# A 32-slot expert, a new order of expert blocks and units, combines in other PSUM banks, and cross attention by all heads at once

## The chip, the cores and the metric

The kernel runs on one core of a Trainium2 chip. The metric is the device time of one execution in microseconds, from the start of the program to its end; lower is better. One execution computes the whole model for one sequence of 256 tokens. Every weight is float32 and is read from HBM once for each use.

## The reference, cut to what matters

Two blocks of two layers each run one after the other, on a sequence of 256 tokens with 1024 features. Layer 0 of the first block isn't touched. Its layer 1 ends in a mixture of 8 experts, each token going to 2 of them:

```
def moe_swiglu(u, router_w, w1, w3, w2):
    top_vals, top_idx = lax.top_k(u @ router_w, 2)
    gates = softmax(top_vals)
    ...  # sorted by expert
    y[e] = (silu(x[e] @ w1[e]) * (x[e] @ w3[e])) @ w2[e]    # w1, w3: 1024 x 2816, w2: 2816 x 1024
    return sum of gates * y over the token's experts
```

Each layer of the second block mixes tokens, adds cross attention to a memory of 256 rows, and ends in 16 experts in groups, of which a token takes two:

```
q = z[..., last 512 columns]                   # z = x @ w_in
s = einsum('bshd,bmhd->bhsm', q, k) * 128 ** -0.5     # 4 heads of 128
o = einsum('bhsm,bmhd->bshd', softmax(s), v)
x = layer_norm(ALPHA * x + concat([tok, o]) @ w_out)
h = silu(xt @ w_gate[e]) * (xt @ w_up[e])      # 1024 x 512 each, 16 experts
out = out + combine[:, e:e + 1] * (h @ w_down[e])
```

`tok` is a spatial gating unit in the first of these layers and a short convolution in the second.

## The kernel before

**The stream of weights.** All large weights come through `raw` (L195 to L203): it takes the next slot of a ring of SBUF slots, and SyncE (SP) issues one DMA into it, of 1024 KB or 768 KB. A slot can be loaded again once TensorE (PE) has done the last matmul that reads it, so an SP that runs ahead waits at the next `dma_start` for PE, and everything behind it on SP waits too.

**Layer 1's experts** (`moe_layer1`). The tokens of an expert are gathered into a fixed number of slots. The first expert is expert 0; the others follow by the number of their tokens. The first five have 96 slots, the last three 64 (`NL = 5`). The columns of one expert's hidden width are cut into three blocks of 1024, 1024 and 768, and a unit (q, i) is block i of the q-th expert. `up` (matmuls at L1234) multiplies the gathered tokens by w1 and w3: with 64 slots, the output of 64 rows uses half of PE's columns, so two matmuls into different halves of the array run side by side; with 96 slots the work is cut into groups of 32 columns, four side by side. `turn` (L1259) transposes the hidden values through PE, and `down` (L1280) multiplies by w2 into `y`, whose banks stay reserved for the expert. PSUM has three banks "g" for `up`, three "y" for `y`, and two "b" for everything small. `combine` (L1285 to L1309) takes a finished expert's `y`, splits it in two terms by ScalarE (`yh`) and VectorE (`yl`), multiplies by the transposed selection on PE and adds the gated result to `macc` on VectorE. Each of its two halves has four matmuls.

The order on PE is written by hand: a unit's `up`, then the `down` of the unit before, then its own `turn`. Two streams of experts, the 96-slot ones and the 64-slot ones, are merged by what remains of each. Where an expert has just finished, half 0 of its combine stands before the `down` of that place and half 1 behind it, in "b" banks.

**Block 2** (`block2`). The layer's input is transposed; `gemm_T` and `gemm_N` multiply by w_in, each weight split in two terms by ScalarE and VectorE (L255, L256) ahead of its matmuls. The generator `cross` (L1504 to L1532) does a head at a time: scores (`xs`), softmax on ScalarE and VectorE (`xp`), transposes (`xpT`), the product with v (`xo`). Two heads are asked for ahead of the last gemm and two behind it; a scheduler places their instructions between those of the gemm. Then w_out, a layer norm, and the router.

**Block 2's experts**. 16 experts are put into seven units of 128 slots. Units 0, 1, 3 and 4 are two experts with 64 slots (12 pieces of weights each), unit 2 is one expert with 128 slots (6 pieces), unit 5 one with 64 and two with 32 (18 pieces), unit 6 four with 32 (24 pieces). They run in this order: the `up` of a unit (L1748), the `down` of the one before (L1774), the combine of the one before that (L1787). The first 16 pieces of the stage are loaded during the mixing ahead of it.

Of the kernel before, what the change touches and what calls it, by code (L numbers as in the profile page):

```python
# [37 lines left out]
KEX = 4  # L38
CAPS = (64,) * KEX + (128,) + (64,) * 5 + (32,) * 6
NL = 5  # L40
# [115 lines left out]
class Net:  # L156
# [1014 lines left out]
    def moe(self, E, F, uh, oh0, rank, slot, gates, w1, w3, w2, acc, mp):  # L1171
# [15 lines left out]
        class Job:  # L1187
# [29 lines left out]
            def up(j, i):  # L1217
# [3 lines left out]
                nb = 3 if m == 96 else 2  # L1221
                ps = [self.bank("up", "g") for _ in range(nb)]

                if m == 96:
                    t, plan = 32, [(0, 0, 0, 0, 0), (0, 1, 0, 0, 32), (0, 2, 0, 0, 64), (0, 3, 0, 1, 64),
                                   (1, 0, 0, 1, 0), (1, 1, 0, 1, 32), (1, 2, 1, 1, 0), (1, 3, 1, 1, 32),
                                   (2, 0, 1, 0, 0), (2, 1, 1, 0, 32), (2, 2, 1, 0, 64), (2, 3, 1, 1, 64)]
                else:
                    t, plan = 64, [(0, 0, 0, 0, 0), (0, 1, 1, 0, 0), (1, 0, 0, 1, 0), (1, 1, 1, 1, 0)]
# [9 lines left out]
                if m == 96:  # L1239
                    parts = [((0, 96), A, (0, 0), (2, 0)), ((0, 64), B, (1, 0), (1, 64)), ((64, 96), B, (0, 96), (2, 96))]  # L1240
                else:
                    parts = [((0, 64), A, (0, 0), (0, 64)), ((0, 64), B, (1, 0), (1, 64))]
# [20 lines left out]
            def down(j, i):  # L1263
# [6 lines left out]
                if m == 96:  # L1270
                    t, one = 32, [(0, 0, 0, 0), (0, 1, 0, 32), (0, 2, 0, 64), (0, 3, 1, 64)]
                    plans = one + [(1, 0, 1, 0), (1, 1, 1, 32)], [(1, 2, 1, 0), (1, 3, 1, 32)] + one
                else:
                    t, plans = 64, ([(0, 0, 0, 0), (0, 1, 1, 0)],) * 2
                v = j.w2[f0:f0 + n, :].rearrange("(p k) d -> p k d", k=nk)
                for k2 in range(0, nk, 2):
                    x = self.raw(v[:, k2:k2 + 2, :], 2, D)
                    for k in range(k2, k2 + 2):
                        for b, c, o, s in plans[k % 2]:
                            nc.tensor.matmul(j.y[b][c * t:(c + 1) * t, :], hT[:, k, s:s + t],  # L1280
                                             x[:, k - k2, o * 512:(o + 1) * 512],
                                             start=(i == 0 and k == (k % 2 if b else 0)), stop=(i == len(blocks) - 1 and k >= nk - 2),
                                             tile_position=(0, c * t), skip_group_check=True)

            def combine(j, halves=(0, 1)):  # L1285
                m, y = j.m, j.y
                for o in halves:
                    js = slice(o * 512, (o + 1) * 512)
                    src = y[0][:m]
                    if o:  # L1290
# [10 lines left out]
                    for tt in range(2):  # L1301
                        p = self.bank("comb")
# [30 lines left out]
        def job(q):  # L1333
# [3 lines left out]
            m = 96 if q < NL else 64  # L1337
# [8 lines left out]
        with tc.manual_schedule(engines={mybir.EngineType.PE}):  # L1346
# [3 lines left out]
            for u, (q, i) in enumerate(units):  # L1350
# [5 lines left out]
                if out is not None:  # L1356
                    jobs[out].combine((0,))
# [18 lines left out]
        nc.vector.tensor_scalar(capv, rank, float(NL), 32.0, op0=OP.is_lt, op1=OP.mult)  # L1376
        nc.vector.tensor_scalar(capv, capv, 64.0, None, op0=OP.add)
        over = mp.tile([128, E], F32, name="over")
# [636 lines left out]
```

## Time and profile before

| | us |
|---|---|
| median of 3 runs (2153.97 to 2158.74) | 2156.89 |
| the profiled execution, its own time | 2155.77 |
| its span in the trace | 2153.9 |
| layer 1's experts, first `up` to last `macc` | 761.9 to 1456 |
| block 2, first layer: mixing and routing | 1456 to 1568 |
| block 2, first layer: experts | 1568 to 1796 |
| block 2, second layer: mixing and routing | 1796 to 1913 |
| block 2, second layer: experts, then the end | 1913 to 2153.9 |

The span is what the trace shows between its first and its last instruction; the execution's own time is 1.9 us longer. The mean granted clock of TensorE was 0.965 of full speed. TensorE is busy for 92% of the span, VectorE for 39%, ScalarE for 27%. The transfers moved 634.57 MB, 294 GB/s over the span, but this mean hides stages with 187 GB/s (the first 762 us) and with over 400.

### The profile page before, as it was taken

How to read it: one execution, taken by the hardware profiler on the slowest of the kernel's cores; microseconds unless marked ns; L12 is line 12 of the kernel's file. 1: busy time of each engine (PE TensorE's matmuls, PEld its weight loads, DVE VectorE, ACT ScalarE, POOL GpSimd, SP SyncE). 2: the span in 40 equal slices, each digit the busy share in tenths (PEclk: the TensorE clock that was granted, in tenths of full speed). 3: DMA queues.
4: the chain of work that ended last, by engine and by line, in shares of the span. 5: the costliest groups of instructions: out<-in, count | busy, mean ns of one | idle time of the engine just before them, and what ended most of it. 6: DMA issues, size and time to landing. Idle time of an engine off the chain costs nothing. (4 is left out here: it accounts for less than half of the span.)

```text
span 2153.9 us, 32324 instructions
## 1 busy us (share of the span) xinstructions
PE 1982.9 (92%) x13265; PEld 1102.5 (51%) x13265; DVE 831.4 (39%) x1703; ACT 577.9 (27%) x973; POOL 82.9 (4%) x121
## 2 busy tenths in 40 slices
PE   6999897999889899999999999998799997989996
PEld 2777665889867533333333333337643425843431
DVE  4464476445778601101211111017632315652223
ACT  3353254334533411101101011015321212522210
POOL 1010100000130000000000000001000001000000
PEclk9999998999999999999999999998899998989998
DMA  7532557784532679999999999976589898479996
GB/s 293 182 119 111 196 176 262 262 274 145 182 100 84 232 290 368 395 410 411 411 390 411 411 408 414 411 308 222 191 340 384 362 421 333 154 304 401 377 391 249
DMA packets 166339, 634.57 MB, mean 295 GB/s; under 512 B 11952, under 2 KB 53040, under 8 KB 124192
## 3 DMA queue, kind: packets, MB, share of 16 engines
q1 hardware_dynamic: 163808, 630.76, 76.2%
q8 instruction: 111, 1.82, 0.3%
q0 software_dynamic: 2080, 1.04, 0.2%
q10 hardware_dynamic: 288, 0.52, 0.1%
q14 instruction: 52, 0.43, 0.1%
HBM read 631.20 MB, written 1.05 MB: 294 GB/s over the span
## 5 line engine op out<-in xcount | busy, mean ns | idle before, releaser
L1234 PE MATMUL up<-raw,xg 128*32 128x512 f32 (+3 forms) x3456 | 403.6, 560 | 0.0
L256 DVE TENSOR_TENSOR wh<-raw,wh 128x1024 fp32r<-128x1024 f32 x182 | 221.3, 1222 | 180.2 <-ACT wh L255 179.0
L1234 PEld LDWEIGHTS up<-raw,xg 128*32 128x32 f32 (+1 forms) x3456 | 133.0, 115 | 255.0 <-issue 248.5
L255 ACT ACTIVATE wh<-raw 128x1024 fp32r<-128x1024 f32 x182 | 190.8, 1058 | 231.6 <-PE gT L192 88.3
L1748 PE MATMUL up<-raw,xg 128*64 128x512 f32 (+1 forms) x1088 | 207.8, 601 | 4.5 <-DMA raw<-in_w_up 2.9
L1280 PE MATMUL y<-raw,hT 128*32 128x512 f32 (+1 forms) x1584 | 208.6, 608 | 0.0
L1246 DVE TENSOR_TENSOR h<-up,h 64x512 f32<-64x512 f32 (+5 forms) x63 | 40.8, 647 | 390.3 <-ACT h L1244 389.5
L1774 PE MATMUL y<-raw,hT 128*64 128x512 f32 (+1 forms) x576 | 133.4, 597 | 8.9 <-DMA raw<-in_w_down 4.1
L1244 ACT ACTIVATE h<-up 64x512 f32<-64x512 f32 (+5 forms) x63 | 35.0, 555 | 371.5 <-PE up L1234 371.0
L1280 PEld LDWEIGHTS y<-raw,hT 128*32 128x32 f32 (+1 forms) x1584 | 60.2, 116 | 139.2 <-issue 126.8
L1748 PEld LDWEIGHTS up<-raw,xg 128*64 128x64 f32 (+1 forms) x1088 | 63.5, 129 | 132.8 <-issue 124.6
L1754 DVE TENSOR_TENSOR h<-up,h 64x512 f32<-64x512 f32 x28 | 29.6, 1056 | 192.2 <-ACT h L1753 192.1
L190 PE MATMUL gT<-fuTh,wh 128*128 128x256 f32 x352 | 101.0, 287 | 0.0
L191 PE MATMUL gT<-fuTl,wh 128*128 128x256 f32 x352 | 99.6, 283 | 0.0
L192 PE MATMUL gT<-fuTh,wh 128*128 128x256 f32 x352 | 99.5, 283 | 0.0
L445 PE MATMUL mod<-raw,cs 128*32 128x512 f32 x384 | 63.0, 693 | 26.0 <-DMA raw<-in_l_mod_w 26.0
L1774 PEld LDWEIGHTS y<-raw,hT 128*64 128x64 f32 (+1 forms) x576 | 38.4, 124 | 94.1 <-issue 65.1
L1753 ACT ACTIVATE h<-up 64x512 f32<-64x512 f32 x28 | 30.0, 1071 | 193.1 <-PE up L1748 193.1
L190 PEld LDWEIGHTS gT<-fuTh,wh 128*128 128x128 f32 x352 | 67.4, 191 | 12.1 <-issue 10.9
L192 PEld LDWEIGHTS gT<-fuTh,wh 128*128 128x128 f32 x352 | 67.5, 192 | 0.4
L191 PEld LDWEIGHTS gT<-fuTl,wh 128*128 128x128 f32 x352 | 67.4, 192 | 0.2
L1260 ACT COPY hT<-hT 128x384 f32<-128x384 f32 (+1 forms) x24 | 10.5, 438 | 165.2 <-PE hT L1259 142.5
(577 smaller groups left out, 3173.4 us busy)
## 6 DMA issues: line engine op xcount, KB each, us to landing
raw<-in_l_moe_w SPq DMA_DIRECT2D x216, 1024.0 KB, 12.8
raw<-in_w_gate SPq DMA_DIRECT2D x64, 1024.0 KB, 8.8
raw<-in_w_up SPq DMA_DIRECT2D x64, 1024.0 KB, 9.3
raw<-in_w_down SPq DMA_DIRECT2D x64, 1024.0 KB, 12.0
raw<-in_l_mod_w SPq DMA_DIRECT2D x48, 1024.0 KB, 6.4
raw<-in_l_moe_w SPq DMA_DIRECT2D x64, 768.0 KB, 12.9
raw<-in_l_ffn_w SPq DMA_DIRECT2D x33, 1024.0 KB, 5.4
raw<-in_l_w_in SPq DMA_DIRECT2D x14, 1024.0 KB, 5.4
```

The lines of the kernel that those rows point to most:

```text
L190: mm(out, l[0], r[0], start=start, stop=False, skip_group_check=True)
L191: mm(out, l[0], r[1], start=False, stop=False, skip_group_check=True)
L192: mm(out, l[1], r[0], start=False, stop=stop, skip_group_check=True)
L255: nc.scalar.activation(hi, x[:, k:k + s, :], AF.Copy)
L256: nc.vector.tensor_tensor(lo, x[:, k:k + s, :], hi.bitcast(F32), OP.subtract)
L445: nc.tensor.matmul(p[32 * j:32 * j + 32, :], self.cs[:, k, :], x[:, 0, j * 512:(j + 1) * 512], start=(k == 0), stop=(k == KC - 1), tile_po ...
L1234: nc.tensor.matmul(ps[b][c * t:(c + 1) * t, :hn], j.xg[:, k, s:s + t], x[w][:, k - k2, half * hn:(half + 1) * hn], start=(k == 0), stop=(k ...
L1244: nc.scalar.activation(h[a:z, js], ps[b1][o1:o1 + z - a, :hn], AF.Silu)
L1246: nc.vector.tensor_tensor(h[a:z, js], ps[b3][o3:o3 + z - a, :hn], h[a:z, js], OP.mult)
L1280: nc.tensor.matmul(j.y[b][c * t:(c + 1) * t, :], hT[:, k, s:s + t], x[:, k - k2, o * 512:(o + 1) * 512], start=(i == 0 and k == (k % 2 if ...
L1748: nc.tensor.matmul(p[o:o + t, :], xg[:, k, c:c + t], pair[w][:, k - k4, :], start=(k == 0), stop=(k == KC - 1), tile_position=(0, o))
L1774: nc.tensor.matmul(y[o][a:a + n, :], hT[:, q * m + a:q * m + a + n], x[e][:, k, o * 512:(o + 1) * 512], start=(q == 0), stop=(q == 3), til ...
```

## The change

- The smallest expert of layer 1 has 32 slots instead of 64 (`SLOTS1`). Its `up` puts w1 and w3 by two halves into one bank, in four groups of 32 columns; its `down` adds even contraction steps into two groups and odd ones into the other two; its combine first adds these two quarters (one ScalarE copy, one VectorE add for each half).
- Layer 1's units begin with two units of the first expert instead of three before the merge, and the second stream is experts 5, 7, 6, with the 32-slot one in the middle instead of 64-slot experts 5, 6, 7.
- The combine of a finished expert moves behind `down`: half 0, then `turn`, then half 1, in the "g" banks of `up`. The last two combines stay as they are.
- Block 2's units run in the order 0, 1, 5, 3, 2, 4, 6.
- Cross attention computes the scores of all four heads into four banks and all softmaxes at the start; the probabilities lie in a slot of the ring (`room`), which goes back behind the fourth head. The heads' transposes and products with v are placed at every second step of the next gemm. In the first layer the scores move ahead of the gemm for v; the transposes `swT` and the row of logits move into the last gemm.

The core of the diff:

```diff
+UNITS = (0, 1, 5, 3, 2, 4, 6)
-NL = 5
+SLOTS1 = (96,) * 5 + (64,) * 2 + (32,)
+SECOND = (5, 7, 6)
...
-                nb = 3 if m == 96 else 2
+                nb = {96: 3, 64: 2, 32: 1}[m]
...
+                    t, plan = 32, [(0, 0, 0, 0, 0), (0, 1, 0, 1, 0), (0, 2, 1, 0, 0), (0, 3, 1, 1, 0)]
...
+                    t, plans = 32, ([(0, 0, 0, 0), (0, 1, 1, 0)], [(0, 2, 0, 0), (0, 3, 1, 0)])
...
-            def combine(j, halves=(0, 1)):
+            def combine(j, halves=(0, 1), tag="b"):
...
+                    if m == 32:
+                        src = mp.tile([128, 512], F32, tag="half", name="ysum", bufs=2)[:m]
+                        nc.scalar.copy(src, y[0][o * 32:o * 32 + 32])
+                        nc.vector.tensor_tensor(src, y[0][64 + o * 32:96 + o * 32], src, OP.add)
...
-        streams = [[(q, i) for q in qs for i in range(nb)] for qs in (range(NL), range(NL, E))]
-        units, streams[0] = streams[0][:nb], streams[0][nb:]
+        streams = [[(q, i) for q in qs for i in range(nb)] for qs in (range(SECOND[0]), SECOND)]
+        units, streams[0] = streams[0][:2], streams[0][2:]
...
                 out, done = done, None
-                if out is not None:
-                    jobs[out].combine((0,))
...
                 if out is not None:
-                    jobs.pop(out).combine((1,))
+                    jobs[out].combine((0,), "g")
                 jobs[q].turn(i)
+                if out is not None:
+                    jobs.pop(out).combine((1,), "g")
...
+        P = []
+        room, slot = self.take([128, 4, 2, 256], F32, "xp")
         for h in range(4):
             ps = self.bank("xs")
...
+            P.append(ps)
+        for h in range(4):
+            ps = P[h]
...
-            p = lp.tile([128, 2, 256], F32, tag="xp", name="xp", bufs=2)
+            p = P[h] = room[:, h]
...
+        yield
+        for h in range(4):
+            p = P[h]
             pt = self.transpose4([p[:, tt, m * 128:(m + 1) * 128] for m in range(2) for tt in range(2)], "xpT")
...
+            if h == 3:
+                self.ring.append(slot)
             yield
...
+                xs = self.cross(qT, kv, mixT, lp)
+                next(xs)
...
-                xs = self.cross(qT, kv, mixT, lp)
-                next(xs)
-                next(xs)
-                self.gemm_N(w, 0, xT, range(2), lambda i, p: nc.scalar.activation(u[:, i, :], p, AF.Gelu))
-                for _ in xs:
-                    pass
...
+                for q, _ in enumerate(self.steps_N(w, 0, xT, range(2), lambda i, p: nc.scalar.activation(u[:, i, :], p, AF.Gelu))):
+                    if q % 2:
+                        next(xs)
...
+        units = [units[i] for i in UNITS]
```

Three places show how instructions move. The first is TensorE in layer 1's experts where the first expert has just finished; `up` and `y` are the matmuls of `up` and `down`, `hT` the transposes of `turn`, `comb` those of a combine. Before:

```order
L1234 MATMUL up<-raw,xg 64x512 x32
L1304 MATMUL comb<-yh,oht 128x512
L1304 MATMUL comb<-yl,oht 128x512
L1304 MATMUL comb<-yh,oht 128x512
L1304 MATMUL comb<-yl,oht 128x512
L1280 MATMUL y<-raw,hT 32x512 x48
L1304 MATMUL comb<-yh,oht 128x512
L1304 MATMUL comb<-yl,oht 128x512
L1304 MATMUL comb<-yh,oht 128x512
L1304 MATMUL comb<-yl,oht 128x512
L1259 MATMUL hT<-cst,h 128x64 x8
L1234 MATMUL up<-raw,xg 32x512 x96
```

And after, at the same place:

```order
L1238 MATMUL up<-raw,xg 32x512 x96
L1288 MATMUL y<-raw,hT 64x512 x16
L1316 MATMUL comb<-yh,oht 128x512
L1316 MATMUL comb<-yl,oht 128x512
L1316 MATMUL comb<-yh,oht 128x512
L1316 MATMUL comb<-yl,oht 128x512
L1265 MATMUL hT<-cst,h 128x96 x8
L1316 MATMUL comb<-yh,oht 128x512
L1316 MATMUL comb<-yl,oht 128x512
L1316 MATMUL comb<-yh,oht 128x512
L1316 MATMUL comb<-yl,oht 128x512
L1238 MATMUL up<-raw,xg 64x512 x32
```

The two halves of the combine stood on either side of the long run of `y`; now only the eight transposes of `hT` lie between them, and the next `up` follows at once. A 64-slot unit also stands a unit earlier.

The second place is TensorE in the first mixing of block 2, in the gemm ahead of w_out; `gN` are the gemm's matmuls, `xs`, `xpT` and `xo` those of one head of the cross attention. Before:

```order
L334 MATMUL xpT<-cst,xp 128x128 x4
L190 MATMUL gN<-wh,xTh 128x512
L191 MATMUL gN<-wh,xTh 128x512
L192 MATMUL gN<-wh,xTl 128x512
L190 MATMUL gN<-wh,xTh 128x512
L191 MATMUL gN<-wh,xTh 128x512
L192 MATMUL gN<-wh,xTl 128x512
L1530 MATMUL xo<-xpTs,mem_4833 128x256 x2
L1512 MATMUL xs<-mem_4833,bq 128x256 x2
```

After, for the second head; the scores of all heads (`xs`, eight matmuls in a row) now stand before the gemm for v, straight behind that for q:

```order
L336 MATMUL xpT<-cst,xp 128x128 x4
L192 MATMUL gN<-wh,xTh 128x512
L193 MATMUL gN<-wh,xTh 128x512
L194 MATMUL gN<-wh,xTl 128x512
L192 MATMUL gN<-wh,xTh 128x512
L193 MATMUL gN<-wh,xTh 128x512
L194 MATMUL gN<-wh,xTl 128x512
L1552 MATMUL xo<-xpTs,mem_4833 128x256 x2
L192 MATMUL gN<-wh,xTh 128x512
```

A head's product with v is no longer followed by the next head's scores, and all four heads lie within the gemm; before, the last two lay within the matmuls of w_out.

The third place is SyncE in block 2's first expert stage, behind the 16 pieces loaded ahead: four `w_down` pieces of unit 0, and what follows. `TENSOR_LOAD` reads the number of an expert whose weights are picked by count, and an `ISA` row belongs to the DMA behind it. Before:

```order
L200 DMA raw<-in_w_down 128x2048 x4
L1799 TENSOR_LOAD idx
L1799 ISA x2
L200 ISA
L200 DMA raw<-in_w_gate 128x2048
L200 ISA
L200 DMA raw<-in_w_up 128x2048
L200 ISA
L200 DMA raw<-in_w_gate 128x2048
L200 ISA
L200 DMA raw<-in_w_up 128x2048
L200 DMA raw<-in_w_down 128x2048 x4
```

After:

```order
L202 DMA raw<-in_w_down 128x2048 x4
L1824 TENSOR_LOAD idx
L1824 ISA x2
L1824 TENSOR_LOAD idx
L1824 ISA x2
L1824 TENSOR_LOAD idx
L1824 ISA x2
L202 ISA
L202 DMA raw<-in_w_gate 128x2048
L202 ISA
L202 DMA raw<-in_w_up 128x2048
```

Before, one expert's four pieces for `up` follow, then the `w_down` of unit 1; now the numbers of three experts are read, and twelve pieces for their `up` come before the `w_down` of unit 1.

## Rows read from the trace of the kernel before

**Rows 1.** The page, busy time and share of TensorE over the span.

```profile
PE 1982.9 (92%) x13265; PEld 1102.5 (51%) x13265; DVE 831.4 (39%) x1703; ACT 577.9 (27%) x973; POOL 82.9 (4%) x121
```

**Rows 2.** By stage: start:end, length, busy PE, PEld, DVE, ACT, POOL; clock, DMA share, GB/s.

```profile
761.90:836.00 74.10, 71.51 (x677) 24.49 (x680) 6.58 (x11) 5.46 (x10) 0.00 (x0) 0.98 0.85 323
836.00:1433.00 597.00, 588.00 (x4636) 209.88 (x4630) 82.07 (x136) 61.23 (x118) 0.00 (x0) 0.99 1.01 406
...
1585.00:1735.00 150.00, 140.61 (x698) 59.29 (x696) 41.39 (x67) 32.06 (x43) 0.00 (x0) 1.00 0.95 387
1735.00:1789.00 54.00, 47.37 (x259) 13.62 (x262) 9.46 (x14) 4.79 (x6) 5.14 (x8) 1.00 1.01 419
...
1930.00:2079.00 149.00, 140.59 (x695) 58.99 (x694) 40.62 (x66) 32.03 (x43) 0.00 (x0) 1.00 0.95 387
```

**Rows 3.** The same view, windows of 100 us within layer 1's experts.

```profile
900.00:1000.00 100.00, 99.27 (x790) 35.98 (x784) 10.51 (x18) 6.68 (x13) 0.00 (x0) 1.00 1.02 411
1000.00:1100.00 100.00, 96.80 (x734) 33.54 (x734) 18.37 (x30) 12.70 (x24) 0.00 (x0) 0.98 1.00 400
...
1300.00:1400.00 100.00, 99.62 (x748) 34.51 (x738) 12.19 (x19) 8.77 (x16) 0.00 (x0) 1.00 1.02 412
```

**Rows 4.** Waits of SP's DMA queue, 761.9 to 1456: us, times, longest.

```profile
SPq L200 <- PE up L1234: 315.5, 126, 9.2
...
SPq L200 <- DMA raw<-in_l_moe_w: 20.6, 19, 2.0
```

**Rows 5.** Groups of PE by shape, 761.9 to 1456: busy us, mean ns, idle before.

```profile
L1234 PE MATMUL up<-raw,xg 128*64 128x512 f32 x384 | 83.7, 594 | 0.0
...
L1280 PE MATMUL y<-raw,hT 128*64 128x512 f32 x264 | 58.6, 596 | 0.0
...
L1234 PE MATMUL up<-raw,xg 128*64 128x384 f32 x192 | 31.6, 488 | 0.0
```

**Rows 6.** Timeline of PE, `up` of a 96-slot and a 64-slot unit: start, us.

```profile
1161.09 20.81 PE L1234 MATMUL up<-raw,xg 128*32 128x512 f32 x192
...
1281.01 13.95 PE L1234 MATMUL up<-raw,xg 128*64 128x512 f32 x64
```

**Rows 7.** Timeline, sum of two parts of `y` in layer 1's last combine.

```profile
1450.05 0.58 ACT L1293 COPY ysum<-y 64x512 f32<-64x512 f32 x1 [12.52 <-PE y L1280]
1450.67 0.68 DVE L1295 TENSOR_TENSOR ysum<-y,ysum 64x512 f32<-64x512 f32 x1 [9.33 <-ACT ysum L1293]
```

**Rows 8.** Waits of PE, 761.9 to 1456: us, times, longest.

```profile
PE xg L1208 <- DVE macc L1308: 4.1, 4, 2.0
...
PE hT L1259 <- DVE macc L1308: 1.9, 5, 0.4
```

**Rows 9.** Timeline of PE, end of block 2's first experts; in brackets the wait before.

```profile
1783.76 1.90 PE L1774 MATMUL y<-raw,hT 128*32 128x512 f32 x4 [0.44 <-DMA raw<-in_w_down]
1786.25 1.90 PE L1774 MATMUL y<-raw,hT 128*32 128x512 f32 x4 [0.59 <-DMA raw<-in_w_down]
1788.73 3.62 PE L1774 MATMUL y<-raw,hT 128*32 128x512 f32 x20 [0.58 <-DMA raw<-in_w_down]
```

**Rows 10.** The page, DMA issues: count, KB each, median us to landing.

```profile
raw<-in_w_gate SPq DMA_DIRECT2D x64, 1024.0 KB, 8.8
```

**Rows 11.** Loads by SP, 1425 to 1573: ns min/median/max, first and last start.

```profile
L200 SPq DMA_DIRECT2D raw<-in_w_up x8: 327/328/340, 1483.1 to 1556.3; - x8
```

**Rows 12.** Waits of PE in block 2's first mixing, 1456 to 1568.

```profile
PE xo L1530 <- ACT xpTs L1527: 1.9, 2, 1.2
PE xpT L334 <- DVE xp L1524: 1.4, 1, 1.4
```

**Rows 13.** Timeline of ACT behind the gemm for q in that mixing.

```profile
1479.51 1.38 ACT L1548 ACTIVATE bq<-gT 128x256 f32<-128x256 f32 x4 [1.05 <-PE gT L192]
```

**Rows 14.** Waits of PE in block 2's second mixing, 1796.3 to 1913.

```profile
PE xpT L334 <- DVE xp L1524: 0.4, 2, 0.2
```

**Rows 15.** Timeline of PE, `up` of four 32-slot experts in block 2.

```profile
1738.39 11.35 PE L1748 MATMUL up<-raw,xg 128*32 128x512 f32 x96
```

More of the change, by code (lines that the diff above doesn't have):

```diff
@@ L1281, in down @@
                                              x[:, k - k2, o * 512:(o + 1) * 512],
-                                             start=(i == 0 and k == (k % 2 if b else 0)), stop=(i == len(blocks) - 1 and k >= nk - 2),
+                                             start=(i == 0 and k == (k % 2 if b or m == 32 else 0)), stop=(i == len(blocks) - 1 and k >= nk - 2),
                                              tile_position=(0, c * t), skip_group_check=True)
-            def combine(j, halves=(0, 1)):
+            def combine(j, halves=(0, 1), tag="b"):
                 m, y = j.m, j.y
@@ L1301, in combine @@
                     for tt in range(2):
-                        p = self.bank("comb")
+                        p = self.bank("comb", tag)
                         for hl in range(2):
@@ L1375, in moe @@
         capv = mp.tile([128, E], F32, name="capv")
-        nc.vector.tensor_scalar(capv, rank, float(NL), 32.0, op0=OP.is_lt, op1=OP.mult)
-        nc.vector.tensor_scalar(capv, capv, 64.0, None, op0=OP.add)
         over = mp.tile([128, E], F32, name="over")
+        nc.vector.tensor_scalar(capv, rank, float(SLOTS1.index(64)), 32.0, op0=OP.is_lt, op1=OP.mult)
+        nc.vector.tensor_scalar(over, rank, float(SLOTS1.index(32)), 32.0, op0=OP.is_lt, op1=OP.mult)
+        nc.vector.scalar_tensor_tensor(capv, capv, 32.0, over, op0=OP.add, op1=OP.add)
         nc.vector.tensor_tensor(over, self.count, capv, OP.subtract)
@@ L1579, in block2 @@
                 self.layer_norm(st, v, sgb, v)
+                next(xs, None)
+                self.ring.append(self.kvs[layer])
                 wo = self.w_out_steps(t["w_out_2"][layer], mixT)
@@ L1607, in block2 @@
                     self.gemm_T(w, 1536, xT, 256, ev_q)
-                self.gemm_T(w, 512, xT, 256, lambda i, p: nc.scalar.activation(cg[:, i, :], p, AF.Copy))
                 xs = self.cross(qT, kv, mixT, lp)
                 next(xs)
-                next(xs)
-                self.gemm_T(w, 0, xT, 256, lambda i, p: nc.scalar.activation(bg[:, i, :], p, AF.Copy))
-                for _ in xs:
-                    pass
+                self.gemm_T(w, 512, xT, 256, lambda i, p: nc.scalar.activation(cg[:, i, :], p, AF.Copy))
+                cf = self.logits_row(gb[:, 1, :], self.rwt[:, 256:512], NE2)
+                for q, _ in enumerate(self.steps_T(w, 0, xT, 256, lambda i, p: nc.scalar.activation(bg[:, i, :], p, AF.Copy))):
+                    if q % 2:
+                        next(xs)
+                next(xs, None)
                 self.gemm_T(w, 1024, xT, 256, ev_x)
                 self.ring.append(self.kvs[layer])
-                cf = self.logits_row(gb[:, 1, :], self.rwt[:, 256:512], NE2)
                 wo = self.w_out_steps(t["w_out_2"][layer], mixT)
@@ L1621, in block2 @@
             uT = self.take([128, KC, 256], F32, "uTf", xp[0])[0]
-            lt = lp.tile([128, 2, 256], F32, tag="xp", name="logT", bufs=2)[:, 0, :]
+            lt = lp.tile([128, 2, 256], F32, tag="xpT", name="logT", bufs=2)[:, 0, :]
             lg = self.lg
```

17 lines of the change are left out of this document (10 added, 7 removed).

## The prediction

> **What bounds the kernel now.** I read the page first: TensorE (PE) is busy for 1982.9 us of the 2153.9 us span [rows 1]. So the question for every stage is whether PE itself or the stream of weights paces it. The table by stage answers it [rows 2]. Its columns to watch are PE's busy time and the last one, GB/s. From 836 to 1433 us, in layer 1's experts, both are near their end at once: PE is busy for 588.00 of 597 us and the queue moves 406 GB/s; five windows of 100 us from 900 on have 400 to 412, the first and the last 411 and 412 [rows 3]. In the two expert stages of block 2 the same stream runs at 387 GB/s early (1585 to 1735, 1930 to 2079) and at 419 in the first one's tail [rows 2]: there the queue has room first and none later.
>
> The queue's waits say who paces it in layer 1 [rows 4]: SP, which issues the loads, waits 315.5 us for PE's `up` matmuls alone to give a slot back, and 20.6 us for a transfer. The list of PE's waits there (two of its lines are [rows 8]) has no transfer in it. So layer 1's experts are PE's, with the queue close behind. In block 2's tail it is reversed: `y` waits for `w_down` [rows 9], and the three rows there start 2.49 and 2.48 us apart, which is one 1 MiB piece at 421 GB/s. So those stages end when the last piece lands.
>
> The profiled execution took 2155.77 us, the median is 2156.89; I sum against 2155.8 and add 1.1 at the end.
>
> **32 slots for layer 1's smallest expert.** From the reference's inputs I counted 13 tokens for it, so 32 slots hold them and the overflow path stays unused. The three 64-slot experts cost PE 83.7 + 31.6 + 58.6 = 173.9 us [rows 5], 58.0 each. Does half the slots mean half the time? A 96-slot block holds 12 column groups per contraction step, three rounds of four, and takes 20.81 us; a 64-slot block holds two rounds of two and takes 13.95 us [rows 6]. A round is 6.94 us with four groups and 6.97 with two: four overlap fully. The 32-slot block is one round, so the expert falls to 29 us: PE gives 29 us. New small work, one ACT copy and one DVE add for each half of its result (0.58 and 0.68 us where the last combine does the same [rows 7]), lies beside PE, except where no matmul is left to hide it; this expert isn't last.
>
> **New order, combining in "g" banks.** Now the gather of the next expert waits for `macc` 4.1 us in 4 times, because its banks are those of the combine, and `hT` for 1.9 [rows 8]. With combines in the three "g" banks these go, 6 us at most. But then the next `up` needs a bank that `macc` must have read, and in several of the new sequences DVE does `yl` of the second half only after it has copied `hT`, while PE stands at that half's matmuls. One link of that chain is a DVE pass of 0.68 us [rows 7]; six experts (the last two still combine in "b") with one or two such links make 4 to 8 us. I take 4 gained less 4 lost, zero, with -6 to +8 for the range.
>
> What can the stage keep of the 29? The queue decides. In 836 to 1433 it moved 597 x 406 = 242 MB; at the 412 of the better windows that needs 588 us, at the 419 of block 2's tail 578 us. So 9 to 19 us can go there before the queue is the bound and PE waits for pieces. A little comes from the start: 762 to 836 runs at 323 GB/s [rows 2], some 15 us of unused queue, of which the earlier second stream (64 slots in the fourth unit rather than the fifth) recovers perhaps 3. I take **-15 us**, nearer the windows of 412 (rows of this very stage) than 419, plus the start. Ends: -5, where the last windows get no faster and the queue's gaps move instead of closing, and -33, where PE keeps all.
>
> The Trainium skill, DMA: Bandwidth & Descriptors, section on bandwidth, gives about 358 GB/s as the limit of HBM for one core and 425 for one core with its neighbour idle. The rows here are above the first and just below the second; by 425 the stage could lose 27 us in place of 15 (an estimate, 597 x (1 - 406/425)), and by 358 nothing at all.
>
> **Block 2's order of units.** Each layer streams 96 pieces of 1 MiB (64 of w_gate in the two layers [rows 10], as many of w_up and of w_down). 16 are loaded ahead: eight of w_up, issued from 1483.1 to 1556.3 [rows 11], and eight of w_gate. The other 80 at 2.49 us need 199 us from the first slot given back, some 5 us after 1568: about 1777 at best, and the last row of [rows 9] starts at 1788.7. The 12 us between are where the queue ran dry: 150 x (1 - 387/421) = 12.1 [rows 2]. That stretch holds unit 2, one expert with 128 slots, which gives back 6 pieces while it does the matmuls of a unit of 12. The new order puts the unit of 18 pieces third and the 6-piece one fifth, so slots come back early and SP gets ahead. The 24-piece unit stays last, so the end stays the queue's. I take 80% of the 12: **-9.5 us**, and the same in the second layer, whose row is alike (387 in 149 us). Ends of each: 0, if the dry stretch only moves later, and -12.
>
> **Cross attention.** In the first of the two layers PE waits 1.9 us for `xpTs` and 1.4 for `xp` [rows 12]: a head's softmax stands between its scores and its transposes with little PE work between. Scores of all heads first, and probabilities ready before the next gemm, take these 3.3 us away. Against that, the scores now stand right behind the q gemm, where the four ACT copies of `bq` (1.38 us for the four [rows 13]) must end first: 0.5 to 0.9 us of wait. **-3 us** (-6 to +1). The second layer has only 0.4 us of such waits [rows 14], so it pays the 0.5 and gains little: **+0.5** (-1 to +3). PE's work is the same, only moved. The other moves: swT, the row of logits and the tag of `logT` go between gemm steps; one DVE operation more in the capacity check is beside PE's 20 us blocks. The cross attention holds one slot of the ring until the last head. A piece or two is therefore issued later, but the last of the 16 goes out at 1556.3 [rows 11], long after the last head, and is used behind 1568, so nothing.
>
> **Sum.** -15 + 0 - 9.5 - 9.5 - 3 + 0.5 = -36.5: 2119.3 for the profiled execution, 2120.4 against the median. I say 2120.
>
> **Rivals.**
> 1. *The queue swallows the expert's saving.* Speaks for it: a DMA share of 1.01 over 836 to 1433 [rows 2] and 1.02 in the windows [rows 3]. Then layer 1 gives -5: 2130. Chance 0.18.
> 2. *PE keeps everything.* Needs 419 GB/s through layer 1 and the unused start: -33 there gives 2155.8 - 33 - 21.5 = 2101.3, or 2102 by the median. Against it: no window of layer 1 passes 412. Chance 0.12. By the 425 of DMA: Bandwidth & Descriptors in the Trainium skill the total would be 2108, an estimate between the forecast and this rival.
> 3. *The order in block 2 only moves the dry stretch.* Unit 2 now runs fifth, and the queue can't go further ahead than the ring's 16 or 17 slots: 0 in both layers gives 2139. Speaks against it: the unit of 18 pieces, now third, gives back half as many slots again as one of 12 for about as many matmuls, so SP enters the 6-piece unit with a longer lead. Chance 0.12.
> 4. *Slower.* The cross attention's slot and the in-order SP: the load that takes that slot waits for PE's last head, and all later pieces stand behind it. Each piece that isn't there at 1568 costs 2.49 us at the stage's end, as it is the queue's. To turn -36.5 takes 36.5 / (2 x 2.49) = 7.3 pieces of 16 in each layer; ten would be 2170. Against it: the slot is back ahead of the w_out matmuls, and the last of the sixteen went out at 1556.3 already before, for other reasons [rows 11]. Chance 0.03.
> 5. *It doesn't do what it says*: the four groups of the 32-slot `up`, all with different weights in one bank, don't overlap. Then the block takes two rounds, nothing is saved, and layer 1 keeps -3: 2132. But a block of block 2 that has 32-column groups with different weights, 96 matmuls, takes 11.35 us [rows 15], 0.118 each, against 13.95 for 64 in [rows 6], 0.218 each: they overlap. Chance 0.03.
>
> **How the numbers follow.** Forecast 0.52, with its own range 2110 to 2128; rivals 0.18, 0.12, 0.12, 0.03 and 0.03. Rival 2 lies at the edge of 2103, half of it outside (0.06); above 2140 lie rival 4 and the upper part of rival 3 (0.03 + 0.05). So 2103 to 2140 leaves out about 0.15. A measurement of this kernel tells 0.2%, 4.3 us, from no change. Faster by more than that: forecast, rivals 1, 2, 3 and 5, less 0.04 for several bad ends at once: 0.93. Within: 0.03. Slower: 0.04.
>
> **What would show it.** Layer 1: the 32-slot `up` block near 7 us; the stage from first `up` to last `macc` near 679 us instead of 694; windows near 415 GB/s; a few `up` or `y` waits for a transfer, some 10 us. Block 2: 400 GB/s or more over the first 150 us of each expert stage, the last piece some 9 us earlier against the stage's start, and waits for `w_down` still in the tail. First cross attention: no wait for `xpTs`. I am wrong if the windows of layer 1 stay at 406 while PE's waits there rise past 20 us (rival 1), if they reach 419 (rival 2), or if a dry stretch of the same size follows the fifth unit (rival 3).

## The result

The changed kernel takes 2127.64 us (median of 4 runs, 2121.58 to 2129.78) against 2156.33: a ratio of 0.9862 with a 95% interval of 0.9839 to 0.9886. A second set of runs gave 2128.04 and again 0.9862 (0.9844 to 0.9881). The gain is 29 us; 36.5 were forecast, and 2127.6 lies at the upper end of the forecast's own range of 2110 to 2128.

The table by stage tells where it came from; the columns are those of [rows 2]. The kernel before, from the first `up` of layer 1's experts to their last combine, then block 2's first mixing, first experts, second experts:

```profile
761.90:1455.40 693.50, 677.87 (x5406) 240.91 (x5406) 96.67 (x159) 70.73 (x135) 0.00 (x0) 0.99 0.98 389
...
1464.50:1568.00 103.50, 91.17 (x475) 74.02 (x475) 69.67 (x154) 46.75 (x75) 7.76 (x10) 0.88 0.61 217
1568.00:1795.90 227.90, 210.77 (x1048) 80.76 (x1048) 58.31 (x102) 41.31 (x55) 5.14 (x8) 0.99 0.94 384
...
1913.00:2138.30 225.30, 210.58 (x1049) 80.87 (x1048) 58.27 (x102) 41.33 (x55) 4.65 (x7) 0.99 0.90 368
```

The same four stages after, and the stretch ahead of them:

```profile
0.00:768.10 768.10, 701.91 (x4645) 543.93 (x4646) 445.33 (x958) 319.78 (x557) 54.19 (x83) 0.95 0.54 186
768.10:1449.20 681.10, 654.78 (x5407) 231.65 (x5406) 97.56 (x162) 71.75 (x137) 0.00 (x0) 0.99 0.99 396
...
1458.50:1554.10 95.60, 86.69 (x477) 71.01 (x477) 69.57 (x151) 43.29 (x72) 8.32 (x10) 0.91 0.65 234
1554.10:1777.90 223.80, 214.30 (x1048) 82.41 (x1048) 59.26 (x104) 42.75 (x56) 5.15 (x8) 1.00 0.97 394
...
1895.30:2112.70 217.40, 209.59 (x1048) 81.64 (x1048) 58.71 (x102) 41.82 (x55) 4.65 (x7) 1.00 0.93 382
```

The second column is the length of a stage. Layer 1's experts lost 12.4 us, the first mixing 7.9, the first experts of block 2 4.1, the second 7.9; the rest is within 0.5 us, but for the stretch ahead, whose instructions on TensorE are the same, in the same order, and which took 6.2 us more in this execution. It comes back below.

What stops TensorE in layer 1 now is told by its waits from 740 to 1460 (us, times, longest), the answer to [rows 8]:

```profile
PE up L1238 <- DMA raw<-in_l_moe_w: 11.7, 13, 1.5
...
PE comb L1316 <- DVE yl L1312: 5.3, 9, 1.0
...
PE y L1288 <- DMA raw<-in_l_moe_w: 0.5, 2, 0.3
```

There was no wait for a transfer; now there are 15, of 12.2 us. The waits of `xg` and `hT` for `macc` are gone. SP shows the other side, as in [rows 4]:

```profile
SPq L202 <- PE up L1238: 212.9, 100, 7.5
SPq L202 <- DMA raw<-in_l_moe_w: 111.1, 85, 2.5
```

SP's waits for transfers rose from 20.6 to 111.1 us: the queue of outstanding loads is now full where TensorE used to hold it back. The timeline of TensorE shows where, around two units of the 32-slot expert (start, us; in brackets the wait before):

```profile
1051.55 7.07 PE L1238 MATMUL up<-raw,xg 128*32 128x512 f32 x64
...
1093.54 3.62 PE L1288 MATMUL y<-raw,hT 128*32 128x512 f32 x32
...
1101.26 1.91 PE L1238 MATMUL up<-raw,xg 128*32 128x512 f32 x12 [0.35 <-DMA raw<-in_l_moe_w]
...
1106.38 1.91 PE L1238 MATMUL up<-raw,xg 128*32 128x512 f32 x12 [1.51 <-DMA raw<-in_l_moe_w]
...
1111.50 3.45 PE L1238 MATMUL up<-raw,xg 128*32 128x512 f32 x12 [1.50 <-DMA raw<-in_l_moe_w]
```

The first 32-slot `up` block takes 7.07 us; the forecast had said near 7. The second needs its eight pieces before they are there and goes on piece by piece, from 1098 to 1115. Windows by stage say how fast the pieces came:

```profile
762.00:836.00 74.00, 70.96 (x645) 25.27 (x647) 7.46 (x12) 7.72 (x14) 0.00 (x0) 1.00 0.82 308
...
1000.00:1200.00 200.00, 187.86 (x1650) 64.06 (x1646) 30.26 (x51) 23.24 (x45) 0.00 (x0) 0.99 1.02 411
```

411 GB/s at a DMA share of 1.02 is the queue's own pace in this stage. The start is as little used as before: the first of these windows begins 6 us ahead of the first `up`, and over the 74 us from that `up` on the rate is 332 GB/s, against 323 in the kernel before.

### The profile page after: what moved, and what is told of

The parts are those of the page before. It is cut to its first block, busy times and chain, and to the rows that moved or that the text cites. A ratio compares the mean times of both kernels' runs of the same rounds, so it can differ in the third digit from the quotient of the medians.

```text
span 2128.0 us, 32365 instructions
## 1 busy us (share of the span) xinstructions
PE 1967.1 (92%) x13265; PEld 1097.8 (52%) x13265; DVE 832.1 (39%) x1706; ACT 577.8 (27%) x973; POOL 83.3 (4%) x121
## 5 line engine op out<-in xcount | busy, mean ns | idle before, releaser
L1238 PE MATMUL up<-raw,xg 128*32 128x512 f32 (+3 forms) x3456 | 393.1, 559 | 11.7 <-DMA raw<-in_l_moe_w 11.7
L1238 PEld LDWEIGHTS up<-raw,xg 128*32 128x32 f32 (+1 forms) x3456 | 126.5, 113 | 263.3 <-issue 231.3
L1288 PE MATMUL y<-raw,hT 128*32 128x512 f32 (+1 forms) x1584 | 198.0, 600 | 1.6 <-ACT h L1250 1.1
L1807 DVE SCALAR_TENSOR_TENSOR yl<-y,gsl,yh 128x512 fp32r<-128x512 f32 x28 | 20.9, 745 | 95.5 <-ACT yh L1806 95.5
```

What stands on the lines that cost most here:

```text
L1238: nc.tensor.matmul(ps[b][c * t:(c + 1) * t, :hn], j.xg[:, k, s:s + t], x[w][:, k - k2, half * hn:(half + 1) * hn], start=(k == 0), stop=(k ...
```

## The experiments

Each starts from the changed kernel. The stage of layer 1's experts means first `up` to last combine, as above.

**The changed kernel again.** No edit.

> The changed kernel once more, beside the experiments. If the 6.2 us that its profile lost ahead of layer 1's experts (first `up` at 768.1 instead of 761.9, the same instructions in the same order on TensorE) are the granted clock of that execution, another profile has the first `up` anywhere from 760 to 769, and the touched stages repeat: 690 us from first `up` of layer 1's experts to the first transpose of block 2, 95.6 us of first mixing, 341 and 214 us behind it. If the change costs something there, 768 again. Time 2122 to 2130.

Its four stages take 680.8, 96.5, 225.8 and 217.6 us, and the first `up` was at 763.9. Over all profiles in which TensorE's instructions ahead of that `up` are the same, it came between 761.9 and 768.5:

```profile
0.00:761.90 761.90, 690.47 (x4641) 537.26 (x4641) 445.47 (x958) 319.02 (x557) 53.94 (x83) 0.97 0.54 187
```

That is e1_cap64, with a mean granted clock of 0.97 in that stretch; the changed kernel's first profile, above, has 0.95 and 768.1. So the 6.2 us are no cost of the change; the profile of the kernel before lay at the short end. That the granted clock makes the difference isn't shown: e9_order_cap64 reached its first `up` at 762.1 with a mean of 0.95, e2_comb_b at 768.5 with 0.96. The four stages repeat within 2 us here and within 2 to 4.5 us over all profiles that have the same instructions in them, which is why the experiments below are read by stage first and by the median second.

**64 slots for the smallest expert.**

```
-SLOTS1 = (96,) * 5 + (64,) * 2 + (32,)
+SLOTS1 = (96,) * 5 + (64,) * 3
...
```

> All of the change, but the smallest expert keeps 64 slots. Theory (the queue swallows much of the saving): the 64-slot expert costs TensorE 23 to 29 us more, of which 12 us come out of waits for transfers, which fall from 12.2 us to under 3; layer 1's stage 8 to 14 us longer than with 32 slots, total 2135 to 2142. Rival (TensorE's time is kept in full, and the missing 17 us of the forecast went into the combine chain): 23 to 29 us longer, total 2150 or more.

2133.77 us, 0.989 (0.9872 to 0.9907): 5.7 us above the changed kernel, a little less than expected. TensorE's list of waits has no transfer in it any more, and the stage is 9.0 us longer than the 680.8 of e0_after:

```profile
761.90:1451.70 689.80, 676.12 (x5406) 240.36 (x5406) 96.73 (x160) 70.80 (x135) 0.00 (x0) 0.99 0.98 391
```

So the 32 slots brought 9 us of TensorE's 29, and the order and the place of the combines together 3.7 (693.5 less 689.8, single profiles; the same stage of the changed kernel spreads over 3.3 us).

**Combines in their old place and banks.**

```
+                if out is not None:
+                    jobs[out].combine((0,))
                 if new:
                     jobs[new].begin()
...
-                    jobs[out].combine((0,), "g")
+                    jobs.pop(out).combine((1,))
                 jobs[q].turn(i)
-                if out is not None:
-                    jobs.pop(out).combine((1,), "g")
```

> All of the change, but the combines of layer 1 where and in which banks they were (half 0 ahead of `down`, half 1 behind it, "b"). Theory (the queue is the bound of that stage): waits of `comb` for `yl` fall from 5.3 to about 2 us, waits of `xg` and `hT` for `macc` come back with 4 to 6 us, and the time is the same within 3 us. Rival (the new place exposes a chain of VectorE on TensorE): 3 to 5 us faster. Third: combining in "g" is worth its 6 us of waits: 4 to 6 us slower.

2129.12 us, 0.9867 (0.9849 to 0.9885): the same. The waits moved much as expected:

```profile
PE up L1238 <- DMA raw<-in_l_moe_w: 7.8, 9, 1.4
...
PE xg L1210 <- DVE macc L1320: 2.0, 1, 2.0
PE comb L1316 <- DVE yl L1312: 1.9, 4, 0.8
```

3.4 us of `yl` waits went; waits of `xg` and `hT` for `macc` came back with 3.9 us (2.0, 1.5 and 0.4); and the stage took 683.0 us. That the combine's move is worth nearly nothing is shown; the forecast had put zero.

**Block 2's units in the old order.**

```
-UNITS = (0, 1, 5, 3, 2, 4, 6)
+UNITS = (0, 1, 2, 3, 4, 5, 6)
```

> All of the change, but block 2's units in the old order. Theory (the new order takes away TensorE's waits for transfers, 5.9 and 4.5 us in the two layers before, and no more, since TensorE's own work fills the rest): first expert stage 4 us longer, second 6 to 8 us, total 2137 to 2140. Rival (the dry stretch only moves): the same within 3 us. Rival of the forecast (the queue alone sets the end): 9.5 us in each, 2146.

2139.14 us, 0.9919 (0.9902 to 0.9935): the order is worth 11 us. The two expert stages:

```profile
1552.00:1778.30 226.30, 208.90 (x1049) 80.36 (x1048) 58.78 (x104) 42.25 (x56) 5.16 (x8) 1.00 0.95 387
...
1893.90:2119.50 225.60, 210.86 (x1049) 80.97 (x1049) 58.33 (x103) 41.39 (x55) 4.67 (x7) 0.99 0.90 368
```

With the new order the second takes 216.8 to 217.6 us in every profile but e1_cap64's (218.9), so 8 us are the order's. The first takes 221.5 to 225.8, so it is 0.5 to 5 us there.

**Cross attention as before.** `cross` and its calls in `block2`, and the tag of `logT`, are those of the kernel before.

```
-                xs = self.cross(qT, kv, mixT, lp)
-                next(xs)
                 u = lp.tile([128, 2, 512], F32, name="bu")
...
+                xs = self.cross(qT, kv, mixT, lp)
+                next(xs)
+                next(xs)
+                self.gemm_N(w, 0, xT, range(2), lambda i, p: nc.scalar.activation(u[:, i, :], p, AF.Gelu))
+                for _ in xs:
+                    pass
...
```

> All of the change, but the cross attention of block 2 as before (a head at a time, behind the v gemm). Theory (the waits for `xp` and `xpTs`, and the slow matmuls around them, are what it took away): first mixing 103 to 104 us instead of 96, second the same 106 to 107, total 7 to 8 us above the changed kernel. Rival of the forecast (only the 3.3 us of listed waits less a new wait behind the q gemm): first mixing 98.5 to 99.5.

2134.96 us, 0.9885 (0.987 to 0.99), 7 us above the changed kernel. The first mixing is back to the length it had:

```profile
1456.40:1559.90 103.50, 91.18 (x477) 74.03 (x477) 69.67 (x154) 46.79 (x75) 7.56 (x10) 0.88 0.60 217
```

So the cross attention is worth 6 to 8.6 us there (the mixing took 94.9 to 97.4 us in all profiles with the new one), and nothing in the second layer: 106.8 against 105.2 to 107.1.

**Fewer loads for the 32-slot expert.** It loads the first pieces of each unit and uses them again, so only layer 1's stage counts.

```
-                    x = [self.raw(w[:, k2:k2 + 2, f0:f0 + n], 2, n) for w in j.w]
+                    if m != 32 or k2 == 0:
+                        x = [self.raw(w[:, k2:k2 + 2, f0:f0 + n], 2, n) for w in j.w]
...
-                    x = self.raw(v[:, k2:k2 + 2, :], 2, D)
+                    if m != 32 or k2 == 0:
+                        x = self.raw(v[:, k2:k2 + 2, :], 2, D)
```

> The changed kernel, but the 32-slot expert of layer 1 loads only the first of the four pairs of pieces of each `up` and the first piece of each `down`, and uses them again; its result is left wrong by that, so block 2's times don't count, only layer 1's stage does. It takes 3 x 6 + 3 x 3 less 2 or so, some 25 pieces or 60 us, out of the queue and leaves TensorE's work as it is. Theory (the queue is what eats the saving): TensorE's waits for transfers (11 to 12 us) vanish and the stage falls from 681 to 667 to 671 us. Rival (the chain of the combines and gathers): waits vanish but reappear elsewhere, stage 678 or more.

One run. The stage, a window of it, and SP's waits in it:

```profile
767.60:1428.60 661.00, 647.99 (x5407) 230.27 (x5406) 97.64 (x162) 71.62 (x137) 0.00 (x0) 0.99 0.94 369
```

```profile
1000.00:1200.00 200.00, 197.47 (x1772) 70.36 (x1768) 34.64 (x58) 24.68 (x48) 0.00 (x0) 0.98 0.92 360
```

```profile
SPq L202 <- PE up L1239: 348.6, 125, 12.1
```

The stage falls to 661.0 us, further than expected, and SP waits for TensorE again. Against 64 slots in the same order this is 689.8 - 661.0 = 28.8 us: what TensorE gives is 29, as worked out, and the queue takes 20 of them back. The expectation had put the queue's share at the 12 us of listed waits. The other 8 us lie in other idle time and, most of them, in time that counts as busy: with the same matmuls TensorE is idle for 13.0 us of the stage instead of 26.3, and busy for 648.0 instead of 654.8. So a matmul group whose pieces trickle in looks busy in the trace while it waits.

**Another order of units.** The list stands in the expectation.

```
-SECOND = (5, 7, 6)
+ORDER = "0.0 0.1 5.0 5.1 0.2 1.0 1.1 5.2 1.2 7.0 2.0 2.1 2.2 7.1 3.0 3.1 3.2 4.0 7.2 4.1 4.2 6.0 6.1 6.2"
...
+        units = [(int(x[0]), int(x[2])) for x in ORDER.split()]
```

> The changed kernel with another order of layer 1's units, with 64-slot units as the third and fourth and two or three 96-slot units between those of the 32-slot expert: 0.0 0.1 5.0 5.1 0.2 1.0 1.1 5.2 1.2 7.0 2.0 2.1 2.2 7.1 3.0 3.1 3.2 4.0 7.2 4.1 4.2 6.0 6.1 6.2. Theory (the queue has room at the start and not where 32-slot units follow each other closely): over 380 GB/s between 762 and 836 instead of 308, waits of `up` for transfers under 4 us, stage 669 to 674 instead of 681. Rival (the queue's total is the bound from the first piece on): same within 2 us. Rival (the stage pays in waits of `xg`, `y` or `comb` for banks what it saves): 677 or more with new waits of over 4 us.

2115.09 us, 0.9801 (0.9782 to 0.9819): some 13 us below the changed kernel, with intervals that don't touch the 0.9844 of its second set. Stage, start and waits:

```profile
763.60:1433.60 670.00, 650.05 (x5406) 231.66 (x5406) 97.40 (x162) 71.50 (x137) 0.00 (x0) 0.99 1.00 401
```

```profile
762.00:836.00 74.00, 70.78 (x583) 23.93 (x583) 8.11 (x14) 6.68 (x13) 0.00 (x0) 1.00 0.90 342
```

```profile
PE y L1288 <- DMA raw<-in_l_moe_w: 5.4, 8, 1.4
...
PE up L1238 <- DMA raw<-in_l_moe_w: 0.9, 1, 0.9
```

The start runs at 342 GB/s, less than expected; counted from the first `up` on it is 344 against the changed kernel's 332. The waits fall to 6.3 us.

**The same order with 64 slots** tells whether the order helps only where the queue binds.

```
-SLOTS1 = (96,) * 5 + (64,) * 2 + (32,)
+SLOTS1 = (96,) * 5 + (64,) * 3
```

> The order of e6_order, but the smallest expert with 64 slots. Theory (with 64 slots TensorE is the bound in any order, and the order is worth something only where the queue is): stage 687 to 691, as with 64 slots in the changed kernel's order (689.8), so the same 32 slots are worth 17 to 21 us in this order and 9 in the other. Rival (the new order is good by itself, by shorter waits of TensorE for the combines): stage 680 or less.

2128.02 us, 0.9877 (0.9854 to 0.9899); the interval overlaps e1_cap64's, whose median is 5.8 us higher. The stage of the profiled run:

```profile
762.10:1443.20 681.10, 666.90 (x5406) 239.73 (x5406) 96.36 (x160) 70.75 (x135) 0.00 (x0) 1.00 0.99 394
```

That is less than the 687 to 691 expected, and 8.7 us less than e1_cap64's 689.8, without any wait for a transfer in either list. But TensorE's busy time fell by 9.2 us (676.12 to 666.90) with the same matmuls, and the granted clock tells why. In e1_cap64 it stands at the lower of its two levels (1.2 instead of 2.4 GHz) in four places, each at or just behind a wait of TensorE of 0.7 to 2.5 us; a window in each:

```profile
787.00:789.00 2.00, 2.00 (x16) 0.65 (x12) 0.00 (x0) 0.00 (x0) 0.00 (x0) 0.50 0.64 255
1272.00:1274.00 2.00, 2.00 (x8) 0.75 (x10) 0.35 (x1) 0.52 (x1) 0.00 (x0) 0.50 1.01 418
1357.00:1359.00 2.00, 2.00 (x10) 0.45 (x13) 1.46 (x2) 0.00 (x0) 0.00 (x0) 0.50 1.04 424
1436.00:1440.00 4.00, 4.00 (x19) 0.93 (x21) 1.50 (x2) 0.00 (x0) 0.00 (x0) 0.50 0.25 94
```

Counted in windows of 1 us these make 17 us at half the clock, which is 8.5 us of work; in e9_order_cap64's stage the clock is at its upper level until 1 us before the end. So the 8.7 us are the clock's. Whether the order keeps it up isn't shown: behind one and the same wait of 2.47 us (the first `hT` for `h`) it fell in e5_few_loads and stayed up in the changed kernel's first profile, and the profiled run was the fastest of the four here (2120.52; the others 2127.24 to 2131.49). The 32 slots are worth 11.1 us in this order by the stages (681.1 less 670.0) and 12.9 by the medians; e6_order's stage has 20 us at the lower level, so the 17 to 21 us that were expected aren't ruled out. The differences above do not rest on this: the stages of the kernel before, e0_after, e1_cap64 and e5_few_loads have 17 to 18 us at the lower level each.

**Only the end of that order**: 4.1 4.2 6.1 6.2 instead of 6.1 4.1 6.2 4.2.

```
+ORDER = "0.0 0.1 0.2 5.0 1.0 5.1 1.1 5.2 1.2 2.0 7.0 2.1 7.1 2.2 3.0 7.2 3.1 6.0 3.2 4.0 4.1 4.2 6.1 6.2"
```

> The changed kernel's order up to 4.0, then 4.1 4.2 6.1 6.2 instead of 6.1 4.1 6.2 4.2: expert 4 ends two units earlier, so one combine instead of two stands behind the last `up`, and the last `down` is a 64-slot one. With 64 slots the order of e6_order was worth 8.7 us without any wait for a transfer; most of that seemed to lie in the last 20 us (granted clock 0.99 instead of 0.83, the last `y` of 72 records 7.93 us instead of 10.3). Theory (the end costs it): stage 675 to 677 instead of 681, waits for transfers unchanged at 10 to 13 us. Rival (the queue's total sets the end): 680 to 681, with more waits for transfers instead.

2122.4 us, 0.984 (0.9826 to 0.9854), 5.6 us below the changed kernel by the medians; the stage is 2.2 us shorter, and the granted clock over its last 20 us is 0.85, against 0.83. The interval overlaps the changed kernel's, whose stage took 680.8 to 684.1 us in four profiles. So the end is worth some 2 us by the stage, which is no more than that spread; the 8.7 us that the expectation set out from were the clock's.

**A 64-slot unit in second place.** Two orders, the second so that expert 0 is combined first. In the first, expert 5's share is overwritten.

```
+ORDER = "0.0 5.0 0.1 5.1 5.2 0.2 1.0 7.0 1.1 1.2 2.0 2.1 2.2 7.1 3.0 3.1 3.2 7.2 4.0 4.1 4.2 6.0 6.1 6.2"
```

> The order of e6_order with the 64-slot expert brought to the second unit: 0.0 5.0 0.1 5.1 5.2 0.2 1.0 7.0 1.1 1.2 2.0 2.1 2.2 7.1 3.0 3.1 3.2 7.2 4.0 4.1 4.2 6.0 6.1 6.2. Theory (what the start still wastes, 342 GB/s in 762 to 836, is to be had): stage 666 to 669 instead of 670.0, if the gather of the second expert is ready in time. Rival (the choice of the second expert, which VectorE works out during the first unit, is late): a wait of TensorE of 5 us or more ahead of the second unit, stage 672 or more.

```
+ORDER = "0.0 5.0 0.1 5.1 0.2 5.2 1.0 1.1 7.0 1.2 2.0 2.1 2.2 7.1 3.0 3.1 3.2 7.2 4.0 4.1 4.2 6.0 6.1 6.2"
```

> The order of e8_order2, changed so that expert 0, whose combine writes the sum and doesn't add to it, is combined ahead of expert 5: 0.0 5.0 0.1 5.1 0.2 5.2 1.0 1.1 7.0 1.2 2.0 2.1 2.2 7.1 3.0 3.1 3.2 7.2 4.0 4.1 4.2 6.0 6.1 6.2. In e8_order2 expert 5's share was overwritten; its stage of 664.4 us counts, its block 2 doesn't. Theory (the start's unused queue is what remains): over 400 GB/s from 762 to 836, stage 664 to 668, total 2109 to 2113 and 2 to 5 us below e6_order. Rival (expert 5 beside expert 0 costs waits for banks): 670 or more.

The second: 74 us from its first `up` on, then its stage:

```profile
776.90:850.90 74.00, 72.61 (x589) 23.76 (x590) 7.85 (x13) 6.33 (x12) 0.00 (x0) 1.00 1.02 412
```

```profile
776.90:1441.70 664.80, 644.12 (x5398) 234.59 (x5398) 96.35 (x160) 70.78 (x135) 0.00 (x0) 0.99 1.02 409
```

The start is filled: 412 GB/s (in the expectation's window, which begins 15 us before the first `up` here, 387). The stages are 664.4 and 664.8 us, 5 us shorter than e6_order's. But the gather of the second expert now stands ahead of the first `up`, for some 2.5 us, and the second order takes 2112.58 us, 0.9791 (0.9777 to 0.9804): 2.5 us below e6_order, with intervals that overlap. Both beat the changed kernel by 13 to 15 us; which is the better can't be told.

**Longer runs in HBM.** w1 and w3 read as 8 KB runs, the same bytes in another place, so the products are others and only layer 1's stage counts.

```
-                j.w = [w.rearrange("(k p) n -> p k n", p=128) for w in ws[:2]]
+                j.w = [w.rearrange("(p k) n -> p (k n)", p=128) for w in ws[:2]]
...
-                    x = [self.raw(w[:, k2:k2 + 2, f0:f0 + n], 2, n) for w in j.w]
+                    x = [self.raw(w[:, KC * f0 + k2 * n:KC * f0 + (k2 + 2) * n].rearrange("p (a n) -> p a n", a=2), 2, n) for w in j.w]
```

> The changed kernel, but the pieces of layer 1's w1 and w3 are read as 8 KB (and 6 KB) runs of HBM for each partition instead of two runs of 4 KB (3 KB); the same bytes in another order, so the result is wrong and block 2's times don't count. It asks why this stage streams at 411 GB/s when block 2 streams at 421 with runs of 8 KB. If it is the length of the runs: 418 to 421 GB/s in the full windows, stage 4 to 10 us shorter, 671 to 677. If not: 411 and 681.

```profile
1000.00:1200.00 200.00, 192.82 (x1717) 67.37 (x1710) 30.36 (x52) 23.20 (x45) 0.00 (x0) 0.98 1.01 417
```

```profile
768.10:1444.80 676.70, 658.36 (x5407) 232.45 (x5406) 97.92 (x162) 71.62 (x137) 0.00 (x0) 0.98 0.97 398
```

One run: 417 to 420 GB/s in the windows and a stage of 676.7 us, 4.4 shorter, though 31 us of it are at the lower clock. So the ceiling of 411 in layer 1 comes from the way in which w1 and w3 are read, two thirds of the stage's pieces (those of w2 had runs of 8 KB all along). The edit makes the runs longer and changes the order of the addresses with them; that it is the length alone is not shown.

## Why the prediction was right, and where its sizes were off

*32 slots.* The mechanism held at both ends: the block takes 7.07 us, TensorE gives 28.8 us when the queue is relieved (e5_few_loads), and the queue takes most of it back. The term of -15 was mis-sized: the stage lost 12.4 us, of which the 32 slots brought 9.0. The step that failed is the queue's pace. The forecast let it come between 412 and 419 GB/s over 597 us, 9 to 19 us, and added 3 from the start. It ran at 411, which by the same sum is 597 x (1 - 406/411) = 7 us, and the start, counted from the first `up`, stayed at 323 to 333 GB/s. The fastest windows of the stage itself were its ceiling already, and the 419 came from pieces that are read in another way (e7_rows8k). By the 425 GB/s of the Trainium skill's DMA: Bandwidth & Descriptors (section on bandwidth) more was to be had; the rows of this stage don't reach it. Rival 1 was half right: the queue took back 20 of 29 us, not 24.

*Order and combines.* Zero was forecast and 3.7 us came. The combines alone make 2.2 us by the two stages (683.0 against 680.8), but e2_comb_b's has 21 us at the lower clock and e0_after's 17, which is 2 us of work, and the medians don't tell the two apart. The 5.3 us of waits for `yl` are the chain that the forecast priced at 4 to 8.

*Block 2's units.* -9.5 was forecast for each layer; -4.1 and -7.9 came, and over all profiles the first lies between -2 and -6. The step that failed is "80% of the 12 us", which took the queue for the only bound. (The sum before it has a slip: 1568 + 5 + 199 is 1772, not 1777; the 5 us between are about what a load takes from issue to landing there, 5.2 at the least.) TensorE's own waits for transfers, 5.9 us in the kernel before, are nearer to what came in the first layer:

```profile
PE y L1774 <- DMA raw<-in_w_down: 2.8, 5, 0.6
PE up L1748 <- DMA raw<-in_w_gate: 1.7, 1, 1.7
...
PE up L1748 <- DMA raw<-in_w_up: 1.4, 1, 1.4
```

After, in the same view and stage, only this is left:

```profile
PE y L1798 <- DMA raw<-in_w_down: 1.8, 3, 0.6
```

TensorE is busy for 214.3 of the 223.8 us, so it is the bound there. A little of the dry stretch did move, as rival 3 had it, to the units behind the 6-piece one:

```profile
1554.10:1688.00 133.90, 128.72 (x623) 49.80 (x623) 35.43 (x68) 27.53 (x36) 0.00 (x0) 1.00 0.98 404
1688.00:1741.00 53.00, 52.04 (x272) 21.46 (x272) 15.79 (x26) 10.81 (x15) 0.00 (x0) 1.00 0.92 360
1741.00:1771.00 30.00, 27.76 (x138) 9.25 (x134) 5.34 (x8) 3.04 (x4) 5.15 (x8) 1.00 1.02 417
```

From 1688 to 1741 the queue has room again (360 GB/s), but TensorE is busy for 52 of 53 us there, and nothing waits. In the second layer 7.9 us are more than its listed waits for transfers (1.3 + 1.4 us, and 1.8 that follow a step of SP), so that sum is no bound either: all listed waits of TensorE together fell from 14.4 to 7.3 us, 2.4 of it in the gathers and 1.2 in `y` for `hT`, and its busy time by 1.0. In the first layer they fell by about as much, but TensorE's busy time rose by 3.5 us (210.77 to 214.30), which isn't explained.

*Cross attention.* -3 was forecast for the first layer and 7.9 us came, outside the range given for the term. The listed waits (3.3 us) are gone, and no new wait stands behind the q gemm. The step that failed is "PE's work is the same, only moved": the matmuls are the same, but TensorE's busy time in the mixing fell from 91.17 to 86.69 us, and most of that is the granted clock. In the kernel before, the clock fell to the lower level behind the waits of the third head, and the scores of the fourth, four records of TensorE, took 1.91 us where those of the third had taken 1.03:

```profile
1508.43 1.03 PE L1512 MATMUL xs<-mem,bq 128*128 128x256 f32 x4
...
1514.72 0.81 PE L334 MATMUL xpT<-cst,xp 128*128 128x128 f32 x4 [1.38 <-DVE xp L1524]
1516.28 1.32 PE L1530 MATMUL xo<-xpTs,mem 128*128 128x256 f32 x4 [0.75 <-ACT xpTs L1527]
1517.39 1.91 PE L1512 MATMUL xs<-mem,bq 128*128 128x256 f32 x4
```

The stretch in the kernel before, and one behind the last head's transposes after the change:

```profile
1516.00:1522.00 6.00, 5.72 (x18) 4.65 (x19) 2.13 (x7) 1.63 (x6) 0.00 (x0) 0.72 0.55 175
```

```profile
1508.00:1514.00 6.00, 6.00 (x27) 4.97 (x27) 2.79 (x3) 2.56 (x4) 0.00 (x0) 1.00 0.96 328
```

With the old cross attention (e4_cross_old) the fall is back, from 1508 to 1512, and no profile with the new one has it there. Over the whole mixing the kernel before and e4_cross_old have 25 us at the lower level, the changed kernel 18, and 7 us at half the clock are 3.5 of the 4.5 us. So the waits cost more than their listed length, through the clock behind them. In the second layer +0.5 was forecast and +0.2 came.

*The slower rival* didn't happen: the 16 pieces were there at the first `up`, and no `up` in block 2 waits for a transfer.

*The sum.* -12.4 - 7.9 - 4.1 - 7.9 is -32.3; the profile shows -25.9 because of the stretch ahead, and the medians -28.7. The 32 slots and block 2's order in both layers brought 13 us less than forecast, the order of layer 1 and the cross attention 8 us more, so by stages the sum is only 4 us short. That they cancel so far is luck. The other 3.6 us between -32.3 and -28.7 lie outside the stages that the terms are about, where the stretch ahead alone varies by 6.6 us.

## What to carry to other kernels

Before a faster unit of work is credited, set TensorE's time against the queue's for the neighbourhood in which it stands: here 20 of 29 us went into a queue that was already at its pace. Spreading the fast units out and putting light ones early, where the queue had room, gave 11 us more. The waits for transfers that the consumer lists are a first guess at what a better order of loads can give, and no bound: 12.2 us of them stood for 20 in layer 1's experts, and 4.5 went with 7.9 in block 2's second layer, while in the first layer 5.9 went with 4. Before two profiles of a stage are compared to a few us, compare the granted clock in both: 17 us at the lower level in one and none in the other made 8.7 us that had seemed to be the order's. For the queue's ceiling take the fastest windows of the same transfers; other pieces may have another one.

## What the runs showed of the hardware

Layer 1's weights stream at 411 GB/s with runs of 4 KB and 3 KB for a partition in w1 and w3 and at 417 to 420 GB/s with 8 KB and 6 KB (e7_rows8k, one run), at a DMA share of 1.01 to 1.02 in both cases; the order of the addresses changed with the length.

The granted clock of TensorE fell to its lower level at some of its short waits (0.7 to 2.5 us) and not at others: four times in e1_cap64's stage of layer 1's experts, not once before the last microsecond in e9_order_cap64's. Behind the waits of the old cross attention it fell in both profiles that have them.

And the same instructions of TensorE over the first 762 us took 761.9 to 768.5 us in different executions, at a mean granted clock of 0.95 to 0.97 that doesn't follow the time, so a change of a few us is read from its stage, not from the span.
